# Opening an mLSTM layer by quarters of the inner dimension, and deferring the closings of its heads

## The chip, the cores and the metric

One core of a Trainium2 chip. Its engines are TensorE (PE: matmuls, with weight loads listed as PEld), VectorE (DVE), ScalarE (ACT), GpSimd (POOL) and SyncE (SP), which here issues the DMA transfers. The metric is the device time of one execution of the whole program in microseconds; the median of three runs of the kernel before is 1912.3 us (1907.47 to 1912.42).

## What is computed

Two sequences, a prompt of 256 positions and a sample of 512, go through the same two-layer encoder of width 1024. The kernel puts them side by side: positions 0 to 255 are the prompt, 256 to 767 the sample.

```python
def trunk(x, c, ...):
    for l in range(DEPTH):
        mod = jax.nn.silu(c) @ adaln_w[l] + adaln_b[l]
        sh1, sc1, g1, sh2, sc2, g2 = [t[:, None, :] for t in jnp.split(mod, 6, axis=-1)]
        h = rmsnorm(x, norm_g[l, 0]) * (1 + sc1) + sh1
        if l % N_MIXERS == 0:
            y = mlstm_mixer(h, mlstm_w_in[j], mlstm_b_gate[j], mlstm_head_g[j], mlstm_w_out[j])
        else:
            y = swa_mixer(h, attn_w_in[j], attn_sink[j], rel_bias, attn_w_out[j])
        x = x + g1 * y
        h = rmsnorm(x, norm_g[l, 1]) * (1 + sc2) + sh2
        x = x + g2 * conv_ffn(h, ffn_w_up[l], ffn_conv_w[l], ffn_conv_b[l], ffn_w_down[l])
    return rmsnorm(x, final_g)
```

Layer 0 has the mLSTM mixer: four heads with queries, keys and values of width 256, gates that run along the sequence in both directions, a root-mean-square norm of each head's output, an output gate (sigmoid) and an output projection. Layer 1 has windowed attention. Every product of fp32 operands is made of three: each operand is split into a high part, rounded, and a low part, the rest, and high x high, low x high and high x low are summed.

## The kernel before

**Layout.** Activations lie with the 1024 model dimensions on partitions, as eight blocks of 128 (`KC`), and positions along the free dimension. `hh` and `hl` (tiles zh and zl in the profile) hold the high and low part of the normed, modulated input. A weight is loaded to a `raw` staging tile (five of them, 512 KB), ScalarE makes its high part `whi` and VectorE its low part `wlo` (`fp_copy_split`, L225 and L226). All matmuls of a product go through `mm`, so they appear as L219.

**Order.** The program is written once in Python, and a scheduler then fixes the order of the instructions on each engine with its own timeline; tile pools with a fixed number of buffers (six `slab`, five `raw`, four PSUM banks `pa` and four `ps`) add waits. Each engine, and SP's queue of transfers, works strictly in that order.

**The start, `first`.** Layer 0 needs the scale and shift of its first norm, a product of the conditioning vector with 2048 columns of `adaln_w`. `adaln` loads these columns in 16 pieces by rows and multiplies each as it comes (32x512 matmuls), then transposes the result. In turn with this, `Norm` runs on the two halves of the sample (`RANGES[0]`, `RANGES[1]`): ScalarE squares (L103), POOL adds five of the eight squares (L107), TensorE sums the remaining three over the partitions (128x2 matmuls against a constant), VectorE and POOL form the root (L125, L126), a matmul broadcasts it, VectorE scales x (L520). Only when all eight blocks of scale and shift are there does `modulate` apply them (L527) and split the result into zh and zl.

**Products of the opening, `mlstm` and `window`.** Three weight units come first: the gates and the two 128-column halves of head 0's queries. `window` runs each over the sample's two halves in 256 columns, then the prompt, whose norm sums all eight squares on TensorE. Head 0's keys follow unit by unit (`gemmT`), in 512 and 256 columns, then its values (`gemmN`).

**Gate chain and heads.** From the gates come scans on VectorE (L632 to L639), a round trip through DRAM (`mrows`) that spreads a row over partitions, and masks added on POOL (L659). For each head, scores of q and k (tile pa) are multiplied by exponentials E and split into PT; these meet the values; VectorE and ScalarE form hs. The closing of a head and sequence follows at once: POOL takes the root of the norm (L773), ScalarE scales hs (L776), TensorE transposes it (L780), VectorE writes it out (L784). After four heads come the output gates (L796, L797).

**Filling.** Two generators are stepped from within this work: `fillp` makes the rest of layer 0's modulation on TensorE (`adaln_g`), `fill` makes all of layer 1's (`adaln_v`), mainly on VectorE (L467, L469: two passes over 1024 columns for each of 48 rows).

## Time and profile before

| | |
|---|---|
| median of three runs | 1912.3 us |
| the profiled execution | 1916.26 us |
| its span, first to last instruction | 1914.1 us |
| mean granted TensorE clock | 0.984 |
| PE busy | 1832.3 us, 96% |
| DVE busy | 1387.7 us, 73% |
| ACT, POOL busy | 908.6 us, 47%; 557.2 us, 29% |

A line of the timeline gives start, duration, engine, source line, operation, output and inputs with their shapes, and in brackets the idle time before it and what ended that. A line of the view by stretches gives the stretch, its length, then busy time and instruction count of PE, PEld, DVE, ACT and POOL, the granted TensorE clock (1.00 is full), the mean busy share of the DMA engines and GB/s. Matmuls are pipelined, so the distance between the starts of two is their cost, and a busy PE may be one that runs slowly.

### The profile page before, as it was taken

The numbers are of one execution on the slowest core, as the hardware profiler recorded it, in microseconds if no ns is written. First come the engines' busy times: TensorE is split into PE (matmuls) and PEld (weight loads), VectorE is DVE, ScalarE is ACT, GpSimd is POOL, SyncE is SP. The second block draws the span as 40 slices with busy tenths as digits, with TensorE's granted clock in tenths as the row PEclk, the third lists the DMA queues.
The fourth block names the chain that finished last, engine by engine and source line by source line (L and its number), as shares of the span: only waits on it lengthen the run. The fifth ranks groups of instructions, "written<-read, shape, count | busy, mean of one in ns | idle before, by whom it ended". The sixth has DMA issues, their size and how long they took to land.

```text
span 1914.1 us, 29110 instructions
## 1 busy us (share of the span) xinstructions
PE 1832.3 (96%) x11270; PEld 1671.3 (87%) x11270; DVE 1387.7 (73%) x2249; ACT 908.6 (47%) x1828; POOL 557.2 (29%) x438
## 2 busy tenths in 40 slices
PE   7999999999999999999999999999899999999997
PEld 4978887879988999999999998779898999999996
DVE  4765577684689777777777765775898777777775
ACT  3444334433555444444444555774564444444443
POOL 2101001022344333333332211332534333333324
PEclk7999999999999999999999999999999999999998
DMA  8344466455212222122223231122222222222211
GB/s 323 113 142 130 148 199 209 159 175 174 70 55 78 67 66 67 66 66 67 66 67 99 84 95 42 46 82 88 78 66 78 67 67 67 66 67 67 67 34 66
DMA packets 63957, 183.43 MB, mean 96 GB/s; under 512 B 6135, under 2 KB 23799, under 8 KB 63820
## 3 DMA queue, kind: packets, MB, share of 16 engines
q1 hardware_dynamic: 63820, 181.58, 29.1%
q8 instruction: 88, 1.44, 0.3%
q14 instruction: 49, 0.40, 0.1%
HBM read 175.13 MB, written 6.43 MB: 95 GB/s over the span
## 4 chain that ended last, share of the span: by engine, by line
PE 83%; DVE 6%; issue 4%; POOL 2%; DMA 2%; ACT 2%; SPq 0%; POOLq 0%; ACTq 0%; DVEq 0%
PE pa L219 26%; PE ps L219 23%; PE ps L1083 10%; PE ps L1084 10%; PE ps L1085 10%; PE pa L941 2%; DVE slab L550 1%; DVE wlo L226 1%; DMA raw<-in_adaln_w_dram 1%; POOL nt L107 1%; PE pa L1083 1%; PE pa L1084 1%; PE pa L1085 1%; ACT whi L225 1%; DMA raw<-in_w_dram 1%
## 5 line engine op out<-in xcount | busy, mean ns | idle before, releaser
L225 ACT CAST whi<-raw 128x1024 fp32r<-128x1024 f32 x243 | 254.6, 1049 | 422.0 <-PE pa L219 204.2
L226 DVE TENSOR_TENSOR wlo<-raw,whi 128x1024 fp32r<-128x1024 f32 x243 | 335.1, 1381 | 137.3 <-ACT whi L225 136.1
L219 PE MATMUL pa<-slab,whi 128*128 128x256 f32 (+1 forms) x1472 | 348.0, 334 | 4.7 <-DVE slab L550 4.6
L219 PEld LDWEIGHTS pa<-slab,whi 128*128 128x128 f32 x1472 | 254.1, 191 | 31.8 <-DVE slab L550 6.2
L550 DVE SCALAR_TENSOR_TENSOR slab<-pa,mod,slab 128x256 f32<-128x256 f32 (+1 forms) x368 | 207.2, 591 | 73.1 <-PE pa L219 73.1
L219 PE MATMUL pa<-slab,wlo 128*128 128x256 f32 (+1 forms) x736 | 234.9, 332 | 0.0
L219 PE MATMUL ps<-zh,whi 128*128 128x256 f32 (+2 forms) x688 | 228.3, 336 | 4.6 <-ACT whi L225 3.5
L219 PE MATMUL ps<-zh,wlo 128*128 128x256 f32 (+2 forms) x688 | 228.4, 335 | 3.4 <-DVE wlo L226 3.4
L219 PE MATMUL ps<-zl,whi 128*128 128x256 f32 (+2 forms) x688 | 229.0, 335 | 0.7 <-DVE zl L513 0.7
L1083 PE MATMUL ps<-zh,whi 128*128 128x384 f32 x504 | 171.0, 339 | 16.2 <-ACT ps L1146 15.2
L1085 PE MATMUL ps<-zh,wlo 128*128 128x384 f32 x504 | 169.0, 335 | 0.0
L1084 PE MATMUL ps<-zl,whi 128*128 128x384 f32 x504 | 168.9, 335 | 0.0
L219 PEld LDWEIGHTS pa<-slab,wlo 128*128 128x128 f32 x736 | 140.1, 191 | 13.0 <-DVE wlo L226 0.6
L1114 POOL TENSOR_TENSOR raw<-raw,raw 128x512 f32<-128x512 f32 x44 | 59.7, 1357 | 312.3 <-DVE wlo L226 263.6
L219 PEld LDWEIGHTS ps<-zh,whi 128*128 128x128 f32 x688 | 131.3, 192 | 17.6 <-ACT whi L225 5.1
L219 PEld LDWEIGHTS ps<-zh,wlo 128*128 128x128 f32 x688 | 131.6, 191 | 14.5 <-DVE wlo L226 4.2
L219 PEld LDWEIGHTS ps<-zl,whi 128*128 128x128 f32 x688 | 131.4, 192 | 11.9 <-issue 1.7
L1235 POOL TENSOR_TENSOR slab<-slab 128x772 f32<-128x772 f32 x44 | 87.5, 1989 | 179.1 <-DVE slab L1186 178.0
L1185 DVE SCALAR_TENSOR_TENSOR slab<-slab,cstt,slab 128x771 f32<-128x771 f32 x88 | 106.7, 1215 | 26.8 <-ACT slab L1183 26.7
L1186 DVE SCALAR_TENSOR_TENSOR slab<-slab,cstt,slab 128x771 f32<-128x771 f32 x88 | 121.0, 1375 | 0.7
L469 DVE SCALAR_TENSOR_TENSOR ada<-raw,silc,ada 128x1024 f32<-128x1024 f32 x84 | 110.3, 1345 | 7.8 <-DMA raw<-in_adaln_w_dram 7.6
L1083 PEld LDWEIGHTS ps<-zh,whi 128*128 128x128 f32 x504 | 94.6, 188 | 24.2 <-ACT ps L1146 20.3
(279 smaller groups left out, 4186.3 us busy)
## 6 DMA issues: line engine op xcount, KB each, us to landing
raw<-in_w_dram SPq DMA_DIRECT2D x206, 512.0 KB, 3.7
raw<-in_adaln_w_dram SPq DMA_DIRECT2D x84, 512.0 KB, 4.3
slab<-in_x_dram SPq DMA_DIRECT2D x12, 512.0 KB, 8.4
slab<-in_adaln_w_dram SPq DMA_DIRECT2D x12, 512.0 KB, 10.3
slab<-mrows SPq DMA_DIRECT2D x8, 384.0 KB, 5.1
xs<-slab SPq DMA_DIRECT2D x6, 512.0 KB, 3.5
bt<-brow SPq DMA_DIRECT2D x16, 192.0 KB, 3.2
slab<-xs SPq DMA_DIRECT2D x6, 512.0 KB, 8.2
```

Source lines behind the costliest of these rows:

```text
L219: self.nc.tensor.matmul(out, lhsT, rhs, start=start, stop=stop)
L225: nc.scalar.copy(hi, src)
L226: return nc.vector.tensor_tensor(lo, src, hi.bitcast(F32), ALU.subtract)
L469: stt(acc[:, s], row, w, acc[:, s], ALU.mult, ALU.add)
L550: self.nc.vector.scalar_tensor_tensor(x, o, self.mod[l][:, gc + c, q : q + 1], x, ALU.mult, ALU.add)
L1083: mm(o, wh[:, k], hi[k], start=start and k == 0, stop=False, skip_group_check=True)
L1084: mm(o, wh[:, k], lo[k], start=False, stop=False, skip_group_check=True)
L1085: mm(o, wl[:, k], hi[k], start=False, stop=k == 3, skip_group_check=True)
L1114: tt(q[0], q[2], q[0], ALU.subtract)
L1185: stt(y[:, 1:], u[:, :-1], w(0), y[:, 1:], ALU.mult, ALU.add)
L1186: stt(y[:, :-1], u[:, 1:], w(2), y[:, :-1], ALU.mult, ALU.add)
L1235: nc.gpsimd.tensor_tensor(y, y, yrow[:, j], ALU.mult)
```

## The change

The modulation's 2048 columns are repacked on the host into an array `ada0` of four quarters; a quarter holds the scale and shift of two of the eight blocks. The sample's x is loaded first, in four transfers, then quarter 0, the gate weight and the two query weights, then quarters 1 to 3, then the prompt's x.

`opening` takes the place of `adaln`, `scaled`, `modulate` and the window. It norms the whole sample at once, with the squares summed on VectorE; other norms keep their sums on POOL. `adaln_z` makes one quarter: eight matmuls, a copy, and four narrow matmuls against a selector `sel` in place of transposes. For each quarter the two blocks are scaled, shifted and split, and the three units are multiplied by these two blocks in 512 columns; the next quarter's modulation matmuls stand between the products of this quarter. Head 0's keys over the sample follow, with the prompt's norm between them (five of its squares are summed on POOL, three sums on TensorE), and then all five units over the prompt. Within `opening`, TensorE, ScalarE and VectorE keep the order in which it is written.

`modulated`, which layer 1's opening norm also uses, writes the low part of a block one block later. A load of ScalarE's exponential table is fixed in program order behind the opening. The closing of a head becomes a generator `close`: the norm's root is taken at once, scale, transposes and write-out later; for the sample behind the prompt's outputs, for the prompt behind the next head's first product (behind the first output gate for the last head). The steps of `fill` and `fillp` are spread anew. The prompt's exponentials are split once per block, not once per direction.

```diff
+    def apart(self, src, pool):
+        w = [[pool.tile([P, 640], R, tag="PT", name=self.nm("wp"), bufs=8)[:, :512] for _ in range(2)] for _ in range(2)]
+        for j in range(2):
+            self.fp_copy_split(w[0][j], w[1][j], src[:, 512 * j : 512 * (j + 1)])
+        return w
...
+    def products(self, o, w, ks, cols):
+        for k in ks:
+            ah, al = self.hh[:, k, cols], self.hl[:, k, cols]
+            self.mm(o, w[0][k], ah, k == 0, False)
+            self.mm(o, w[0][k], al, False, False)
+            self.mm(o, w[1][k], ah, False, k == KC - 1)
+    def opening(self, xt, units, loads, pool, consume):
+        nc = self.nc
+        stt = nc.vector.scalar_tensor_tensor
+        sample = slice(*SEQS[0])
+        x = lambda c: xt[c // 4][:, c % 4, sample]
+        ws, bank = [], []
+        acc = None
+        for c in range(KC):
+            sq = pool.tile([P, 640], F32, tag="PT", name=self.nm("sq"), bufs=8)[:, :512]
+            nc.scalar.activation(sq, x(c), AF.Square)
+            if acc is None:
+                acc = sq
+            else:
+                nc.vector.tensor_tensor(acc, acc, sq, ALU.add)
+        pm = self.pa()
+        for b in range(4):
+            self.mm(pm[:, 2 * b : 2 * b + 2], acc[:, b * P : (b + 1) * P], self.inv, True, True)
+        r = self.nt.tile([P, 4], F32, tag="nr", name=self.nm("nr"), bufs=3)
+        mean = pm[:, :8].rearrange("p (b s) -> p b s", s=2)[:, :, 0]
+        nc.vector.tensor_scalar(r, mean, EPS, None, ALU.add)
+        nc.gpsimd.tensor_tensor(r, r, self.mhalf[:, :4], ALU.pow)
+        turn = self.adaln_z(0, units[0], pool)
+        next(turn)
+        pr = self.pa()
+        for b in range(4):
+            self.mm(pr[:, b * P : (b + 1) * P], r[:, b : b + 1].to_broadcast([P, P]), self.ident, True, True)
+        for _ in range(2):
+            next(turn)
+        for z in range(4):
+            cs = (2 * z, 2 * z + 1)
+            if z == 0:
+                ws.append(self.blocks(self.apart(loads[0], pool)))
+            for c in cs:
+                stt(x(c), x(c), self.gain[0][0][:, c, 0:1], pr, ALU.mult, ALU.mult)
+            for c in cs:
+                sh = self.mod[0][:, c, 0:1]
+                hi = self.hh[:, c, sample]
+                nc.scalar.activation(hi, x(c), AF.Identity, bias=sh)
+                stt(self.hl[:, c, sample], x(c), sh, hi.bitcast(F32), ALU.add, ALU.subtract)
+            if z < 3:
+                turn = self.adaln_z(z + 1, units[z + 1], pool)
+            for i in range(3):
+                if z == 0:
+                    bank.append(self.ps())
+                    if i:
+                        ws.append(self.blocks(self.split(loads[i])))
+                self.products(bank[i], ws[i], cs, sample)
+                if i == 0 and z < 3:
+                    for _ in range(2):
+                        next(turn)
+                if i == 1 and z < 3:
+                    next(turn)
+        norm = Norm(self, xt, PROMPT, self.modulated(0, 0))
+        for c in range(KC):
+            norm.square(c)
+        stages = norm.stages()
+        next(stages)
+        for i in range(2):
+            w = self.load(U_MIN + 1, i)
+            ws.append(self.blocks(self.apart(w, pool) if i else self.split(w)))
+        for i in range(3):
+            consume[i](0, bank[i])
+        bank += [self.ps() for _ in range(2)]
+        self.products(bank[3], ws[3], range(4), sample)
+        next(stages)
+        self.products(bank[3], ws[3], range(4, KC), sample)
+        consume[3](0, bank[3])
+        for _ in stages:
+            pass
+        self.products(bank[4], ws[4], range(KC), sample)
+        consume[4](0, bank[4])
...
+    def quarter_loads(self, z, pool):
...
+            self.nc.sync.dma_start(part, self.io["ada0"][:, u * 1024 : (u + 1) * 1024])
+            out.append(part.rearrange("p (k c) -> p k c", k=2))
+        return out
+    def adaln_z(self, z, units, pool):
...
+        ps = self.pa()
+        for k in range(KC):
+            r0 = 32 * (k % 4)
+            self.mm(ps[r0 : r0 + 32], self.silc[:, k, :], units[k // 2][:, k % 2], k < 4, k > 3)
+            if k == 3:
                 yield
...
+        sb = pool.tile([P, 640], F32, tag="E", name=self.nm("sb"), bufs=2)
+        nc.scalar.copy(sb[:, :512], ps)
+        yield
+        pt = self.pa()[:, :8]
         for b in range(4):
+            self.mm(pt[:, 2 * b : 2 * b + 2], sb[:, b * P : (b + 1) * P], self.sel, True, True)
+        src = pt.rearrange("p (i b s) -> p i b s", i=2, b=2)
+        for i in range(2):
+            c = 8 * i + 2 * z
...
+            ts = []
+            for c in range(KC + 1):
+                if c < KC:
+                    ts.append(self.tmp([P, c1 - c0]))
+                    g = self.gain[l][i][:, c, q : q + 1]
+                    nc.vector.scalar_tensor_tensor(ts[c], x(c), g, pr, ALU.mult, ALU.mult)
+                    nc.scalar.activation(self.hh[:, c, c0:c1], ts[c], AF.Identity, bias=self.mod[l][:, 24 * i + c, q : q + 1])
+                if c:
+                    b = c - 1
+                    self.behind = nc.vector.scalar_tensor_tensor(
+                        self.hl[:, b, c0:c1], ts[b], self.mod[l][:, 24 * i + b, q : q + 1],
+                        self.hh[:, b, c0:c1].bitcast(F32), ALU.add, ALU.subtract,
+                    )
             return ()
         return apply
...
+        nc.gpsimd.memset(B[0:G], 0.0)
...
-        qt0 = self.slab([P, 2, 2, T], R)
-        ws = [(gw, gates)] + [(w, keep(qt0, 0, c)) for c, w in self.halves(U_MIN)]
-        self.load_x(io["x"], RANGES[2:], xt)
+        qk0 = [self.slab([P, 2, 2, T], R) for _ in range(2)]
+        consume = [gates] + [keep(qk0[i], i, c) for i in range(2) for c in range(2)]
+        eng = mybir.EngineType
+        with self.tc.manual_schedule(engines={eng.PE, eng.Activation, eng.DVE}):
+            ws = opening(consume)
+        behind = self.behind
+        self.tc.keep_in_program_order(
+            nc.scalar.preload_act_table_set("natural_log_exp_and_others")
+        )
         nc.sync.dma_start(self.kct[:, P:], io["kc"][:, P : 3 * P])
-        norm = Norm(self, xt, PROMPT, self.modulated(0, 0), KC)
-        for c in range(KC):
-            norm.square(c)
-        self.start(PROMPT, norm.stages())
-        self.window(ws)
-        nc.scalar.preload_act_table_set("natural_log_exp_and_others")
+        for w, f in zip(ws, consume):
+            o = self.ps()[:, :256]
+            self.products(o, w, range(KC), slice(*SEQS[1]))
+            f(1, o)
...
-                if h == 0 and i == 0:
-                    qk.append(qt0)
+                if h == 0:
+                    qk.append(qk0[i])
                     continue
...
                 for c, w in self.halves(U_MIN + 3 * h + i):
                     for q in range(2):
                         keep(t, i, c)(q, self.gemmT(w, q))
-                        if h and (q <= c or h > 1):
+                        if closes:
+                            self.step(closes.pop(0))
+                        if q <= c or h > 1:
                             self.step(self.fill)
-                    if h:
-                        self.step(self.fillp)
+                    self.step(self.fillp)
                 qk.append(t)
...
-                    if t % 2 == 0:
-                        self.step(self.fill)
-                    elif h:
-                        self.step(self.fillp)
+                    if h:
+                        self.step((self.fill, self.fillp)[t % 2])
...
-                        for d, cols in ((0, slice(nb, w)), (1, slice(0, nb))):
-                            m = cols.stop - cols.start
-                            pts[q, j, d] = [self.tmp([P, m], R) for _ in range(2)]
-                            self.fp_copy_split(*pts[q, j, d], E[:, cols])
+                        t = [self.tmp([P, w], R) for _ in range(2)]
+                    self.fp_copy_split(t[0][:, :w], t[1][:, :w], E[:, :w])
+                    pts[q, j, 0] = [x[:, nb:w] for x in t]
+                    pts[q, j, 1] = [x[:, :nb] for x in t]
...
+            def close(h, q, hq, ss):
+                s0, s1 = SEQS[q]
+                t0, t1 = s0 // P, s1 // P
+                nc.vector.tensor_scalar(ss[:, t0:t1], ss[:, t0:t1], 1.0 / 256.0, EPS, ALU.mult, ALU.add)
+                nc.gpsimd.tensor_tensor(ss[:, t0:t1], ss[:, t0:t1], self.mhalf[:, : t1 - t0], ALU.pow)
+                yield
+                for ti, hs in enumerate(hq, t0):
+                    nc.scalar.activation(hs, hs, AF.Copy, scale=ss[:, ti : ti + 1])
+                for c in range(2):
+                    pt = self.pa()
+                    for i, hs in enumerate(hq):
+                        nc.tensor.transpose(pt[:, i * P : (i + 1) * P], hs[:, c * P : (c + 1) * P], self.ident)
+                    ch = 2 * h + c
+                    nc.vector.tensor_scalar(
+                        hsT[ch // 4][:, ch % 4, s0:s1], pt[:, : s1 - s0], self.cst(HG + ch), None, ALU.mult
+                    )
...
                 n = (s1 - s0) // P
-                self.step(self.fillp, 2)
+                self.step(self.fillp)
...
-                    hs = pool.tile([P, 256], F32, tag="hs", name=self.nm("hs"), bufs=4)
+                    if q == 0:
+                        hs = pool.tile([P, 256], F32, tag="hs", name=self.nm("hs"), bufs=4)
+                    else:
+                        hs = self.tmp([P, 256])
...
+                closes.append(close(h, q, hq, ss))
+                next(closes[-1])
+                if q:
+                    self.step(closes.pop(0))
+                with self.tc.issue_after(behind.ins):
+                    self.step(self.fill)
...
                     o = self.gemmT(w, q)
-                    self.step(self.fill)
+                    if closes:
+                        self.step(closes.pop(0))
+                    self.step((self.fill, self.fillp)[q])
+                    if q and c:
+                        self.step(self.fill)
...
+        xt = [self.slab([P, 4, T]) for _ in range(2)]
+        for c in range(0, KC, 2):
+            t0, t1 = SEQS[0]
+            self.nc.sync.dma_start(xt[c // 4][:, c % 4 : c % 4 + 2, t0:t1], x[:, c : c + 2, t0:t1])
+        self.sel = pool.tile([P, 2], F32, name="sel")
+        self.nc.vector.tensor_reduce(
+            self.sel, self.ident.rearrange("p (g s) -> p s g", g=4)[:, 0:2], op=ALU.add, axis=mybir.AxisListType.X
+        )
+        units = [self.quarter_loads(0, pool)]
+        loads = [self.raw(self.io["wg"])] + [self.load(U_MIN, c) for c in range(2)]
+        units += [self.quarter_loads(z, pool) for z in (1, 2, 3)]
+        self.load_x(x, RANGES[2:], xt)
...
+    a0 = inp["adaln_w"][0][:, :2048].reshape(KC, P, 2, 4, 256)
+    arr["ada0"] = np.ascontiguousarray(a0.transpose(1, 3, 0, 2, 4).reshape(P, 4 * 4096))
```

134 lines of the change are left out of this document (29 added, 105 removed).

## The prediction

> **What bounds the kernel now.** I read the page's shares of engine time first, then the chain of work that ended last, then the stretches (busy time of each engine, granted TensorE clock, DMA).
>
> ```profile
> PE 1832.3 (96%) x11270; PEld 1671.3 (87%) x11270; DVE 1387.7 (73%) x2249; ACT 908.6 (47%) x1828; POOL 557.2 (29%) x438
> ...
> PE 83%; DVE 6%; issue 4%; POOL 2%; DMA 2%; ACT 2%; SPq 0%; POOLq 0%; ACTq 0%; DVEq 0%
> ```
>
> ```profile
> 0.00:10.00 10.00, 0.00 (x0) 0.00 (x0) 0.46 (x4) 5.45 (x11) 2.38 (x7) 1.00 0.78 264
> 10.00:20.00 10.00, 9.47 (x48) 3.13 (x48) 2.90 (x9) 0.01 (x1) 2.17 (x3) 1.00 1.02 391
> 20.00:30.00 10.00, 7.02 (x30) 3.17 (x28) 3.37 (x3) 3.66 (x9) 4.26 (x6) 0.70 1.03 414
> 30.00:40.00 10.00, 9.20 (x49) 5.11 (x41) 7.33 (x24) 4.28 (x14) 0.08 (x1) 0.67 1.05 397
> 140.00:160.00 20.00, 16.03 (x105) 13.26 (x104) 8.85 (x24) 10.62 (x33) 8.98 (x6) 0.91 0.53 161
> 160.00:400.00 240.00, 235.17 (x1671) 202.85 (x1670) 166.78 (x284) 96.81 (x253) 19.43 (x12) 1.00 0.52 170
> 400.00:500.00 100.00, 96.01 (x546) 87.26 (x545) 56.45 (x79) 32.57 (x58) 23.88 (x19) 0.97 0.44 148
> 500.00:1914.00 1414.00, 1361.54 (x8158) 1267.10 (x8156) 1071.84 (x1705) 710.05 (x1356) 489.07 (x383) 0.99 0.22 69
> ```
>
> TensorE carries 83% of the chain. A change pays where TensorE has no useful work or runs at a lower clock: the first 45 us, where the DMA runs full (391 to 414 GB/s) and few matmuls run, the end of the first head (16.03 busy of 20), and 4.8 and 4.0 us of idle in 160:400 and 400:500. After 500 us the changed kernel's instruction lists are the same but for a few places around layer 1's opening norm, so I give that stretch nothing. The opening in the timeline, TensorE's lines mainly:
>
> ```profile
> 13.36 1.69 PE L219 MATMUL pa<-inv,nt 128*128 128x2 f32 x12
> 14.97 1.06 PE L219 MATMUL ps<-raw,silc 128*32 128x512 f32 x8
> 15.08 0.16 DVE L125 TENSOR_SCALAR nr<-pa 128x2 f32<-128x2 f32 x1 [13.78 <-PE pa L219]
> 16.09 0.71 PE L219 MATMUL pa<-kct,nr 128*128 128x128 f32 x4
> 23.23 3.20 PE L219 MATMUL ps<-slab,silc 128*32 128x512 f32 x8 [2.89 <-DMA slab<-in_adaln_w_dram]
> 29.02 1.93 PE L219 MATMUL ps<-slab,silc 128*32 128x512 f32 x8
> 38.42 5.28 PE L219 MATMUL pa<-inv,nt 128*128 128x2 f32 x24
> 40.72 1.04 ACT L225 CAST whi<-raw 128x1024 fp32r<-128x1024 f32 x1
> 43.57 0.56 PE L219 MATMUL ps<-zh,whi 128*128 128x256 f32 x1
> 44.40 1.22 DVE L226 TENSOR_TENSOR wlo<-raw,whi 128x1024 fp32r<-128x1024 f32 x1
> 62.06 0.28 PE L219 MATMUL ps<-zh,whi 128*128 128x256 f32 x1
> 63.14 0.28 PE L219 MATMUL pa<-zh,whi 128*128 128x256 f32 x1
> 71.66 0.28 PE L219 MATMUL pa<-zh,wlo 128*128 128x256 f32 x1
> 72.94 0.39 PE L219 MATMUL ps<-zh,whi 128*128 128x512 f32 x1
> 77.25 0.39 PE L219 MATMUL ps<-zl,whi 128*128 128x512 f32 x1
> ```
>
> Products run steadily from 43.57; at 63.14 the three opening units (gates and the two halves of head 0's queries) are done for the sample sequence and those of the prompt begin. From 62.06 to 71.66 stand 80 matmuls of 256 columns, 0.12 us apart; from 72.94 to 77.25, 19 of 512, 0.227 apart. The clock:
>
> ```profile
> 24.00:34.00 10.00, 9.92 (x42) 4.67 (x44) 3.25 (x8) 1.04 (x1) 2.09 (x3) 0.50 1.04 398
> 38.00:48.00 10.00, 9.94 (x46) 9.65 (x47) 10.00 (x28) 7.46 (x21) 0.89 (x1) 0.50 0.46 165
> 44.00:46.00 2.00, 2.00 (x11) 2.00 (x11) 2.00 (x5) 1.46 (x5) 0.00 (x0) 0.50 0.00 0
> 50.00:52.00 2.00, 2.00 (x20) 2.00 (x19) 0.00 (x0) 0.00 (x0) 0.40 (x1) 1.00 0.59 217
> ```
>
> At clock 0.50 eleven products go in 2 us, at 1.00 twenty. Products from 43.57 on brought the full clock back at about 48, 4.4 us later.
>
> **The change, part by part.** *Landing of the transfers.* The opening stays bound by DMA, so I carry the bytes over: 2.64 MB moved by 10 us, 6.55 by 20, 10.69 by 30, 14.66 by 40. The transfer TensorE awaited at 23.23 is the 13th of 0.52 MB (7.15 MB with the constants) while 7.9 MB had moved: one lands when 0.74 MB more than its own sum have moved. New order: sample x (2.43 MB), quarter 0 (4.53), gate and two query weights (6.10), quarters 1 to 3 (8.20, 10.3, 12.4), prompt x. Landings: x 11.4, quarter 0 16.7, gate weight 18.1, quarter 1 25.8, quarter 3 36.1 us. The three weights, moved ahead of quarter 1 on SP's queue, cost that quarter 1.57 MB, 3.8 us.
>
> *Up to the first product.* Eight squares of 512 on ScalarE with the sums on VectorE follow the landings. VectorE's and ScalarE's times for 512 columns are those of the old sample evictions:
>
> ```profile
> 60.46 0.60 ACT L228 ACTIVATE slab<-ps 128x512 fp32r<-128x512 f32 x1 [1.50 <-PE ps L219]
> 63.06 0.68 DVE L229 SCALAR_TENSOR_TENSOR slab<-ps,slab 128x512 fp32r<-128x512 f32 x1
> ```
>
> After x: two squares 1.2, last sum 0.7, eight passes of the column sum 1.1 (12 took 1.69), root and its way to TensorE 1.35 (1.0 from 15.08 to 16.09, and by my estimate a third more for four columns instead of two), broadcast 0.7: 16.5. Quarter 0's last part 16.7 + 0.5; copy 0.8; eight selecting passes 1.1; three small VectorE steps 0.6: 19.7. Ahead of the modulation VectorE's list has two halves of the gate weight's split, 1.3; then modulation 0.7 and the cast 0.6: first product at **22.4** instead of 43.57. The low parts come 0.8 and 1.5 later, so the first six products end at 24.3.
>
> *Four quarters, TensorE in written order.* Behind the first six stand quarter 1's modulation matmuls (landing 25.8), behind those the products of the second unit. ScalarE has the copy of that modulation ahead of the query weight's cast: 26.3 + 0.8 + 1.04 = 28.1, VectorE's low part 29.4. TensorE did little from 17 to 28, so I take clock 0.50 there, as the row 24:34 has it: second unit until 31.1, selection 1.8 until 32.9, third weight's low part only at 34.7, third unit until 36.4, quarter 1's first unit until 39.0. From 34.7 TensorE is dense, so the clock is full from about 39. A quarter then costs 18 x 0.227 + 1.06 + 1.1 = 6.3 us, and 1.1 of waiting for scale, cast and low part in a row (selection to first product 2.1, covered by the third unit's 1.36): 46.4 after quarter 2's first unit, 53.8 after quarter 3's, **56.5** at the end of the three units, against 63.1: -6.6.
>
> *Rest of the opening.* Before, from 63.1: 72 x 0.12 for the prompt and 16.7 for the key weights = 25.3. After, from 56.5: 48 x 0.227 for the keys, 120 x 0.12 for the prompt = 25.3, plus the prompt's column sums, now in this stretch, 1.7, the broadcast 0.5, and the key weight's low part 0.5. Opening: **-3.9**. Ends: if the clock is full all along, 3 us better; if semaphore hops that I took as 0.1 to 0.2 are double, 3 worse.
> *Nothing for* two things with a cover:
>
> ```profile
> 7.66 3.94 POOL L107 TENSOR_TENSOR nt<-nt,nt 128x256 f32<-128x256 f32 x5 [7.22 <-ACT nt L103]
> 70.46 1.28 ACT L626 ACT_TABLE_LOAD   x1
> 85.27 0.68 DVE L639 TENSOR_TENSOR_SCAN slab<-slab 4x256 f32<-4x256 f32 x1
> 109.25 4.46 PE L219 MATMUL pa<-slab,slab 128*128 128x512 f32 x18
> ```
>
> The prompt's squares now have five sums on POOL; the key products and ScalarE's casts lie over them, bare they are 3.9. The table load at 70.46 stands in the gate chain and goes, but TensorE's products lie over that chain (last scan done at 86, first score at 109). Its new place: the gates are out at 76, scans by 96, masks 106, weights of head 0 split by 116, while TensorE reaches the outputs at about 120. If that cover is gone the whole lateness counts (rival 2). Fewer splits of the scores (8 instead of 16 for the prompt) and a memset moved to POOL lie on engines with room. The later low parts in the shared modulation: one 0.4 us step either way.
>
> *Closings.* Where TensorE waited from the first head's end to the end of the stage:
>
> ```profile
> PE pa L780 <- ACT hs L776: 3.9, 2, 3.3
> PE ps L219 <- DVE wlo L226: 3.4, 4, 1.4
> PE ps L219 <- ACT whi L225: 2.6, 2, 1.4
> ```
>
> The 3.3 is the first head's sample closing: the norm's scale, then transposes. Deferred, it has the prompt's outputs in front (18 x 0.12 = 2.2), so about 1.5 us remain; the clock dip there (0.91 over 20 us, 1.8 us) should halve: **-2.5** (ends 0 and -5.1). The next waits are for weight splits at later heads' ends, 6.0 us, where VectorE and ScalarE now do closing work. The change takes some of it away but adds filling steps there: 39 of the layer-1 modulation's 49 steps are called before the output gates, 34 now. I take **-2** (ends -6 and +8).
>
> Sum: 3.9 + 2.5 + 2 = 8.4. The profiled execution took 1916.3 (span 1914.1); the median is 1912.3, 0.2% under it. 1912.3 - 8.4 = **1904**.
>
> **The rivals.** *1, slower: the splits queue behind the filling.* Each filling step is two VectorE instructions:
>
> ```profile
> L469 DVE SCALAR_TENSOR_TENSOR ada<-raw,silc,ada 128x1024 f32<-128x1024 f32 x72 | 95.4, 1355 | 0.8 <-DMA raw<-in_adaln_w_dram 0.7
> ```
>
> Five more steps are 5 x 2 x 1.36 = 13.6 us more on VectorE in the heads, in less time, and each holds one of five staging buffers that the next weights need. If all of it ends as waits for splits at three heads' ends, -6.4 + 13.6 = +7: 1919. It decides once these waits pass 18 us in place of 6. Against it: VectorE is busy 167 of 240 us in 160:400.
>
> *2, the gate chain takes the opening's gain.* Head 0's weights come at 116 against TensorE's 120: 4 us of slack, and scans wait in VectorE's queue behind splits and filling. If they come 8 us later, the opening's 3.9 is gone and 1908 is left.
>
> *3, the clock stays at half through the quarters.* The waits of 1 us in each quarter, the narrow selections and the DMA could keep it down. From 39.0 on TensorE's 4.9 + 6.3 + 4.1 us of work would double, less 2 of covered waits: +13, so 1917. Against it: eleven half-speed products per 2 us did release it. The Trainium skill, "TensorE: Matmul & The Clock Gate", section "HAM oscillation", speaks for this rival: bursts of matmuls shorter than the wait for the next slice are re-throttled at every slice. By that rule each quarter would start cold, which is the 1917 above. The trace agrees as far as idle time goes: the clock fell to 0.50 by 24 us after the 2.9 us wait ahead of 23.23; but the waits I count after 36 are about 1 us.
>
> *4, more is freed.* The clock is full in the opening (-3) and all waits at heads' ends go (-6): 1895.
>
> *5, the change doesn't do what it says:* only the sample's opening norm moves its sums to VectorE; the other norms' lists still add on POOL. That is counted as nothing above and changes no time.
>
> **How the numbers follow.** Forecast 0.42, rival 4 0.20, rival 1 0.16, rivals 2 and 3 0.11 each. What a measurement of this kernel can tell from no change is about 0.3%, 5.7 us: 1906.6 to 1918.0. Faster: the forecast and rival 4, 0.62; same: rivals 2 and 3, 0.22; slower: rival 1, 0.16. Range 1891 to 1916: from rival 4 with 4 us more for the closings' own bound, up to just under rivals 1 and 3; the forecast's own is 1898 to 1908.
>
> **What would show it.** First product near 22 and the three units done near 56; clock 0.50 until about 39, 1.00 afterwards; key products for the prompt done near 84.5; first outputs of head 0 near 120 without a wait for the score weights; the transposes' wait at most 1.5 us; waits for weight splits in the heads under 6 us. Wrong if the quarters cost over 8 us each, if TensorE waits for head 0's weights, or if the waits for splits pass 15 us.

## The result, and the profile after

The changed kernel took **1932.9 us** (median; 1932.9 to 1934.2) against 1912.4 for the kernel before: 1.0115 times as long, interval 1.0097 to 1.0132. A second measurement beside later experiments gave 1929.2 us and 1.0088 (1.0059 to 1.0118). Forecast were 1904 us and a gain. The sign was wrong, and the time lies outside the range.

The page of the changed kernel shows TensorE with nearly the same busy time and the same place at the head of the chain (80% against 83%); VectorE's share of the chain rose from 6% to 8%:

```profile
PE 1835.4 (95%) x11190; PEld 1666.7 (86%) x11190; DVE 1383.2 (72%) x2224; ACT 907.0 (47%) x1806; POOL 554.4 (29%) x433
...
PE 80%; DVE 8%; issue 3%; ACT 3%; POOL 3%; DMA 2%; SPq 0%; POOLq 0%; ACTq 0%; DVEq 0%
```

To say where the time went, I use one row that both kernels have: the first column sums of the norm that follows layer 0's output projection. Up to there the two programs differ; behind it their instruction lists are the same but for a few places. First the timeline of before, then of the changed kernel:

```profile
490.69 2.06 PE L219 MATMUL pa<-inv,nt 128*128 128x2 f32 x18
```

```profile
509.94 2.06 PE L219 MATMUL pa<-inv,nt 128*128 128x2 f32 x18
```

I call this start S. It came 19.3 us later (a second profile of the changed kernel has 509.7), and the whole span is 17.0 longer (1931.1 against 1914.1). So the loss was made before S. The stretches of the changed kernel (length; busy time of TensorE, weight loads, VectorE, ScalarE, GpSimd; granted clock; DMA share; GB/s):

```profile
30.00:40.00 10.00, 7.54 (x32) 4.22 (x24) 2.49 (x5) 2.48 (x3) 0.00 (x0) 0.67 0.97 370
40.00:50.00 10.00, 9.67 (x44) 6.20 (x45) 3.64 (x9) 1.97 (x3) 0.00 (x0) 0.75 0.18 54
...
160.00:400.00 240.00, 229.63 (x1564) 196.06 (x1564) 157.43 (x269) 89.92 (x233) 14.08 (x10) 0.98 0.47 153
400.00:500.00 100.00, 93.84 (x566) 81.59 (x566) 57.90 (x79) 34.82 (x65) 26.83 (x20) 0.98 0.58 185
```

TensorE's idle time in 160:400 grew from 4.8 to 10.4 us and in 400:500 from 4.0 to 6.2, although VectorE was busy for less of 160:400 than before (157.4 against 166.8). More waiting with no more work: the order in the queues has to be read, not the shares. The granted clock counts too: it stands at 0.98 in 160:400 where the kernel before had 1.00.

**The opening.** TensorE's timeline of the changed kernel:

```profile
13.57 1.86 PE L219 MATMUL pa<-inv,sq 128*128 128x2 f32 x8 [13.57 <-DVE sq L334]
17.23 2.08 PE L219 MATMUL pa<-kct,nr 128*128 128x128 f32 x8
21.90 1.05 PE L219 MATMUL pa<-sel,sb 128*128 128x2 f32 x8 [0.74 <-ACT sb L481]
26.09 0.79 PE L219 MATMUL ps<-zh,wp 128*128 128x512 f32 x1 [3.14 <-ACT zh L358]
33.83 0.50 PE L219 MATMUL ps<-zh,whi 128*128 128x512 f32 x1 [1.66 <-ACT whi L225]
59.85 0.50 PE L219 MATMUL ps<-zh,wp 128*128 128x512 f32 x1 [0.57 <-ACT zh L358]
92.09 0.28 PE L219 MATMUL ps<-whi,zh 128*128 128x256 f32 x1
```

The first product came at 26.09 instead of the forecast 22.4, the last quarter's first at 59.85, and head 0's values (whi,zh) began at 92.09. I call the start of the values V. In the kernel before, V came 3.0 us sooner:

```profile
89.06 0.39 PE L219 MATMUL ps<-whi,zh 128*128 128x256 f32 x1 [0.46 <-DVE slab L226]
```

ScalarE's timeline of the changed kernel at the second unit:

```profile
32.25 0.59 ACT L481 COPY sb<-pa 128x512 f32<-128x512 f32 x1 [5.55 <-PE pa L219]
32.73 2.00 ACT L225 CAST whi<-raw 128x1024 fp32r<-128x1024 f32 x2
```

ScalarE stood idle for 5.55 us ahead of the copy of quarter 1's modulation, and the cast of a weight that could have been made meanwhile is written behind that copy. TensorE then waited for the cast (1.66 at 33.83).

**The heads.** The chain of what held the end of this stage, by line, for before (60 to 490 us) and then for the changed kernel (60 to 510):

```profile
by line: PE ps L219 57.4%; PE pa L219 13.7%; issue 13.0%; DMA raw<-in_w_dram 1.9%; DMA raw<-in_adaln_w_dram 1.6%; PE pa L780 1.3%; DVE wlo L226 1.1%; POOL slab L659 0.9%; DVE ada L469 0.8%; DMA slab<-mrows 0.8%; ACT whi L225 0.7%; DVE ada L
```

```profile
by line: PE ps L219 56.6%; PE pa L219 10.1%; issue 6.6%; DVE ada L558 5.4%; DMA raw<-in_adaln_w_dram 5.0%; DMA raw<-in_w_dram 2.4%; DVE wlo L226 1.7%; DVE slab L839 0.9%; ACT whi L225 0.9%; PE pa L837 0.8%; DVE ada L556 0.8%; ACT nt L103 0.
```

"ada" is the filling (layer 1's modulation on VectorE), "raw<-in_adaln_w_dram" its transfers. In the entries shown, L469 before and L558 after, they went together from 2.4% of the chain to 10.4%. The chain puts down to a transfer all its time from issue to landing, and VectorE can do other work in that time, so such a share is not what VectorE waited. One place, between the second and third heads' ends: the chain's entry, then VectorE's timeline, then TensorE's row in the same view.

```profile
262.87 6.02 DMA raw<-in_adaln_w_dram
```

```profile
259.98 2.48 DVE L558 SCALAR_TENSOR_TENSOR ada<-raw,silc,ada 128x1024 f32<-128x1024 f32 x2 [0.51 <-DMA raw<-in_adaln_w_dram]
...
264.28 2.48 DVE L558 SCALAR_TENSOR_TENSOR ada<-raw,silc,ada 128x1024 f32<-128x1024 f32 x2 [1.21 <-DMA raw<-in_adaln_w_dram]
...
268.98 2.48 DVE L558 SCALAR_TENSOR_TENSOR ada<-raw,silc,ada 128x1024 f32<-128x1024 f32 x2 [1.89 <-DMA raw<-in_adaln_w_dram]
...
271.58 0.68 DVE L810 TENSOR_TENSOR E<-pa,E 128x512 f32<-128x512 f32 x1
```

```profile
272.32 0.97 PE L219 MATMUL pa<-slab,slab 128*128 128x256 f32 x6 [3.50 <-DVE E L810]
```

Three filling steps stand close together on VectorE, with evictions between them. VectorE stood 0.51, 1.21 and 1.89 us for their transfers, and behind the third step stand the products of the third head's score weights (E), for which TensorE waited 3.50 us. A step fetches the row of the next step when it runs, so steps that follow closely stand for their rows. Over the first 520 us the group of these instructions shows, for before and then for the changed kernel, equal work but twice the standing:

```profile
L469 DVE SCALAR_TENSOR_TENSOR ada<-raw,silc,ada 128x1024 f32<-128x1024 f32 x84 | 110.3, 1345 | 7.8 <-DMA raw<-in_adaln_w_dram 7.6
```

```profile
L558 DVE SCALAR_TENSOR_TENSOR ada<-raw,silc,ada 128x1024 f32<-128x1024 f32 x84 | 109.6, 1338 | 15.3 <-DMA raw<-in_adaln_w_dram 15.2
```

TensorE's waits in the changed kernel from 92 to 510 us (sum, times, longest); from head 0's end on, weight splits take no more than before (4.4 + 1.6 against 3.4 + 2.6), and evictions (L229), a modulation transfer and score weights (2.3 us at head 0, 3.5 at the third head) have joined them:

```profile
PE pa L219 <- DVE E L810: 5.8, 2, 3.5
PE ps L219 <- DVE wlo L226: 4.4, 6, 1.8
PE ps L219 <- DVE slab L229: 3.4, 2, 2.4
PE ps L219 <- DMA raw<-in_adaln_w_dram: 2.1, 1, 2.1
PE ps L219 <- ACT whi L225: 1.6, 3, 0.8
```

From V to S the two kernels have the same number of TensorE instructions, 2604 (the second row counts two more at its edges). Before, then the changed kernel (length, TensorE's busy time, clock, DMA share, GB/s):

```profile
89.06:490.69 401.63, 387.10 (x2604) 0.99 0.50 163
```

```profile
92.09:509.94 417.85, 395.68 (x2606) 0.98 0.49 159
```

The 16.2 us lost here have three visible parts. TensorE's idle time is 7.6 us longer (22.2 against 14.5). The clock stood at 0.50 for 20.5 us instead of 10.2, which by my estimate costs up to 5 us. And the narrow products of layer 0's modulation, called at new places too, kept TensorE busy 2.7 us longer; they stand in 30 groups instead of 22:

```profile
L219 PE MATMUL ps<-raw,silc 128*32 128x256 f32 x256 | 19.5, 386 | 0.0
```

```profile
L219 PE MATMUL ps<-raw,silc 128*32 128x256 f32 x256 | 22.2, 396 | 2.1 <-DMA raw<-in_adaln_w_dram 2.1
```

### The profile page after: what moved, and what is told of

Same layout as the page of the kernel before. It is cut to its first block, busy times and chain, and to the rows that moved or that the text cites. A ratio compares the mean times of both kernels' runs of the same rounds, so it can differ in the third digit from the quotient of the medians.

```text
span 1931.1 us, 28919 instructions
## 1 busy us (share of the span) xinstructions
PE 1835.4 (95%) x11190; PEld 1666.7 (86%) x11190; DVE 1383.2 (72%) x2224; ACT 907.0 (47%) x1806; POOL 554.4 (29%) x433
## 4 chain that ended last, share of the span: by engine, by line
PE 80%; DVE 8%; issue 3%; ACT 3%; POOL 3%; DMA 2%; SPq 0%; POOLq 0%; ACTq 0%; DVEq 0%
PE pa L219 25%; PE ps L219 23%; PE ps L1181 10%; PE ps L1182 9%; PE ps L1183 9%; PE pa L1039 2%; DVE wlo L226 1%; DVE ada L558 1%; DMA raw<-in_adaln_w_dram 1%; DMA raw<-in_w_dram 1%; DVE slab L631 1%; POOL nt L107 1%; ACT whi L225 1%; PE pa L1181 1%; PE pa L1182 1%
## 5 line engine op out<-in xcount | busy, mean ns | idle before, releaser
L219 PE MATMUL ps<-zh,whi 128*128 128x256 f32 (+2 forms) x656 | 223.2, 344 | 8.5 <-ACT whi L225 4.2
L219 PE MATMUL ps<-zh,wlo 128*128 128x256 f32 (+2 forms) x656 | 222.7, 342 | 5.7 <-DVE wlo L226 5.7
L219 PE MATMUL ps<-zl,whi 128*128 128x256 f32 (+2 forms) x656 | 223.2, 341 | 0.7 <-DVE zl L605 0.7
L219 PEld LDWEIGHTS ps<-zh,whi 128*128 128x128 f32 x656 | 126.4, 194 | 26.6 <-ACT whi L225 7.4
L219 PEld LDWEIGHTS ps<-zh,wlo 128*128 128x128 f32 x656 | 126.8, 194 | 19.4 <-DVE wlo L226 8.7
L219 PEld LDWEIGHTS ps<-zl,whi 128*128 128x128 f32 x656 | 127.1, 194 | 11.8 <-issue 1.7
L558 DVE SCALAR_TENSOR_TENSOR ada<-raw,silc,ada 128x1024 f32<-128x1024 f32 x84 | 109.6, 1338 | 15.3 <-DMA raw<-in_adaln_w_dram 15.2
L1181 PEld LDWEIGHTS ps<-zh,whi 128*128 128x128 f32 x504 | 94.9, 188 | 25.0 <-ACT ps L1244 21.2
## 6 DMA issues: line engine op xcount, KB each, us to landing
slab<-in_ada_dram SPq DMA_DIRECT2D x12, 512.0 KB, 10.2
```

The lines of the kernel that those rows point to most:

```text
L219: self.nc.tensor.matmul(out, lhsT, rhs, start=start, stop=stop)
L558: stt(acc[:, s], row, w, acc[:, s], ALU.mult, ALU.add)
L1181: mm(o, wh[:, k], hi[k], start=start and k == 0, stop=False, skip_group_check=True)
```

## The experiments

Two numbers are given for each: the median over the runs with its ratio to before on the same chip (interval in brackets), and S of the profiled execution, which says how much of the time lies before the common part. From S to the end the profiles took 1416 to 1429 us with nearly the same instructions, at mean clocks of 0.979 to 0.990, so a single total says less than S. S itself carries the clock of the opening, so V is given beside it: before and closings_only have the same instructions in the same order on every engine up to V, yet V is 89.1 in one and 87.0 in the other, where the clock didn't fall at 24 us.

**Which part costs it.** Four kernels with parts exchanged (the edits are cut to a few lines). With the old opening the heads of the change were put into the kernel before.

```diff
 # open_alone: in the changed kernel
-                    self.step(self.fillp)          # fill/fillp calls, closings and
-                closes.append(close(h, q, hq, ss)) # split of E as in the kernel before
+                for _ in close(h, q, hq, ss):
+                    pass
 # fill_back: only the fill/fillp calls as before; close_back: only the closings as before
```

> The changed opening with the heads, the closings, the filling steps and the splits of the scores as before. Theory O (the opening itself, by its half clock and the late gate chain, costs the 20 us): 1928 or more. Theory F (the filling steps at their new places cost some 15 us, the opening 4): about 1916. Theory C (the deferred closings cost 15): about 1916 too.

> The opening as before with the changed heads (closings deferred, filling steps at their new places, merged splits). Theories F and C: about 1928, the old 1912 and some 15. Theory O: 1912 to 1916, the heads cost next to nothing.

> The changed kernel with the filling steps called where they were before, all else changed. Theory F: 1916 to 1919. Theories O and C: 1930 or more.

> The changed kernel with every closing done at once at its head's end, all else changed. Theory C: 1917 to 1920. Theories F and O: 1930 to 1936, and by the prediction's step on closings (-2.5) 1935.

Two more complete the table on the old opening:

> The kernel before with closings deferred and the prompt's splits merged, filling steps and opening as before. By the prediction's step: 1910 (-2.5). By the part runs (closings add some 2 us at the new opening with old filling): 1912 to 1915.

> The kernel before with the filling steps at their new places, all else as before. If the new places uncover the filling by themselves: 1918 to 1924, start of the output norm 496 or later. If it needs the deferred closings or the new opening: 1912 to 1915.

| opening | closings deferred | filling at new places | V, us | S, us | median, us | ratio |
|---|---|---|---|---|---|---|
| old | no | no (before) | 89.1 | 490.7 | 1911.6 to 1914.3 | 1 |
| old | yes | no (closings_only) | 87.0 | 487.7 | 1910.4 | 0.9991 [0.9975, 1.0007] |
| old | no | yes (filling_only) | 91.5 | 491.8 | 1920.0 | 1.0036 [1.0019, 1.0053] |
| old | yes | yes (heads_alone) | 91.7 | 497.8 | 1918.8 | 1.0037 [1.0021, 1.0053] |
| new | no | no (open_alone) | 96.1 | 492.3 | 1920.8 | 1.0048 [1.0031, 1.0064] |
| new | yes | no (fill_back) | 95.1 | 494.7 | 1917.5 | 1.0032 [1.0013, 1.0051] |
| new | no | yes (close_back) | 90.1 | 497.8 | 1921.3 | 1.0043 [1.0029, 1.0057] |
| new | yes | yes (changed kernel) | 92.1 | 509.9 | 1932.9 | 1.0115 [1.0097, 1.0132] |

(The merged split of the prompt's scores goes with the deferred closings in the old-opening rows and in the last three.) None of the three theories holds: each part put back takes 12 to 18 us of S off, and no part alone costs that much. At S the parts do not add: on the old opening closings and filling together cost 497.8 - 487.7 - 491.8 + 490.7 = 9 us more than the sum of both, on the new one 9.7; counted from V to S, so without the opening, 6.7 and 6.8. The deferred closings by themselves show -3.0 at S, but 2.1 of it stands at V already, ahead of any closing; 0.8 is left behind V, and the total resolves neither. New places of the filling move two things, layer 1's modulation on VectorE and the narrow products on TensorE: the group of 256 takes 19.3 or 19.5 us in the four kernels with the old places and 21.8 to 22.4 in the other four. No run takes one of them alone to its new places. The totals of open_alone and filling_only lie some 4 us higher than their S lets expect; that isn't explained (open_alone's profiled execution, 1912.6, was the fastest of its ten).

**Is it the filling, and what of it?** One kernel thins the filling's work on VectorE, one removes its transfers, one holds it out of head 0's gate chain; the changed kernel was measured again beside them.

```diff
 # thin_fill
-                    stt(acc[:, s], row, w, acc[:, s], ALU.mult, ALU.add)
+                    stt(acc[:, s, :128], row[:, :128], w, acc[:, s, :128], ALU.mult, ALU.add)
 # no_transfers
-        fetch = lambda grp, k: self.raw(self.io["adaln_w"][...])
+        fetch = lambda grp, k: self.hh[:, 0:2, :512].bitcast(F32)
 # gate_clear: every self.step(self.fill) of the heads
+                    if h == 0:
+                        behind = last        # the last product with E on VectorE
+            with self.tc.issue_after(behind.ins):
```

> The changed kernel once more, as the yardstick of the runs beside it, since each of the four part runs lies only 0.3 to 0.5% over before: 1928 to 1936 under every theory.

> The changed kernel, each accumulating VectorE instruction of the filling (layer 1's modulation) on 128 of its 1024 columns, transfers unchanged; the modulation is left incomplete. Theory D (the filling's time on VectorE, 1.28 us an instruction, holds the gate chain and the weight splits): 1911 to 1917. Theory T (its transfers, which hold staging buffers that the weights need, and which VectorE awaits in order): 1926 or more.

> The changed kernel, the filling's VectorE instructions at full size but reading resident data, so its 48 transfers and their staging buffers are gone (the modulation is not computed). Theory T: 1911 to 1917. Theory D: 1926 or more. If both this and the thin filling come to 1917, the two act together (an instruction stands and waits for a late transfer).

> The changed kernel with no filling step before the last score product of head 0 on VectorE. If the filling does its harm in head 0's gate chain (five steps stand there, the first scores' products wait 5.8 us): 1921 to 1926. If it does it at the later heads' ends: 1930 or more.

| kernel | V, us | S, us | median, us | ratio |
|---|---|---|---|---|
| changed kernel again | 92.4 | 509.7 | 1929.2 | 1.0088 [1.0059, 1.0118] |
| thin_fill | 90.1 | 491.5 | 1915.5 | 1.0021 [1.0003, 1.0038] |
| no_transfers | 92.7 | 502.6 | 1922.4 | 1.0057 [1.0039, 1.0075] |
| gate_clear | 90.9 | 509.5 | 1931.5 | 1.0110 [1.0088, 1.0131] |

Taking away either half of the filling brings S forward: 18.4 us without most of its time on VectorE (2.0 of them at V already), 7.3 without its transfers. The two overlap, since their sum is more than the whole 19.3. Theory D fits the larger part; no_transfers fell between the two forecasts. How long VectorE stands for the transfers is not the measure of the harm: in thin_fill it stood 29.9 us for them, twice as long as in the changed kernel, and S is 491.5.

In gate_clear no step stands before head 0's score weights, and TensorE's wait for them (2.3 of the 5.8 us that the expectation put there) is gone. S is unchanged even so: at the first head's end TensorE now waits 8.5 us in five pieces (144 to 157 us) where the changed kernel waits 3.1. So taking the steps out of the gate chain alone gains nothing; the waits came back later.

**Was it hidden before?** The same thinning in the kernel before:

> The kernel before with each accumulating filling instruction on 128 of 1024 columns; the modulation is left incomplete. If the filling was hidden before (theory U: the change uncovers it): 1907 to 1912, start of the output norm 486 to 491. If it cost as much before: 1893 to 1898, start near 472.

S 478.3, median 1900.7 us, ratio 0.9936 [0.9917, 0.9955]. So the filling wasn't hidden before either: its VectorE time was worth 12.4 us of S there and is worth 18.4 now. Neither forecast of this run holds; the change made a cost larger that was there already. But the pair says more. With the filling thinned in both, the changed kernel is still 13.2 us later at S (491.5 against 478.3), and 12.1 of that lies between V and S (thin_before, then thin_fill):

```profile
88.94:478.29 389.35, 382.35 (x2605) 1.00 0.51 168
```

```profile
90.07:491.49 401.42, 389.37 (x2607) 0.99 0.50 164
```

So what the filling's VectorE time costs more than before accounts for 6.0 of the 19.3 us at S, 4.2 of the 16.2 behind V. In the thinned pair TensorE's idle time is 5 us longer in the changed kernel (12.1 against 7.0), and its narrow products take 23.6 us instead of 19.5.

**Does it help to hold the steps back?** Each step was ordered behind the eviction or split written just before its call.

```diff
 # pinned
+            with self.tc.issue_after(self.last.ins):   # last low part written on VectorE
                 self.step(self.fill)
```

> The changed kernel, each filling step of the heads and output gates ordered on VectorE behind the low part of the eviction or split written just before its call; number of steps and their transfers unchanged. Theory H (the scheduler draws steps forward, where they stand with late transfers ahead of weight splits, score products and closings): 1911 to 1918, the start of the output norm near 495 instead of 509.9. If the steps cost the same wherever they stand: 1927 or more, the start near 510.

S 520.8, median 1942.5 us, 1.0160 [1.0135, 1.0185]: worse by 11 at S. My theory H, that the scheduler does the harm by drawing steps forward, fell. VectorE stands 0.0 us for the filling's transfers in this kernel, the slowest at S so far, so that standing isn't the cause either. TensorE's waits in this kernel from 125 to 480 us have other names again:

```profile
PE ps L219 <- ACT whi L225: 6.4, 5, 2.7
PE ps L219 <- DMA raw<-in_adaln_w_dram: 6.1, 2, 3.3
PE pa L845 <- ACT nt L841: 3.0, 3, 1.8
```

**Without VectorE.** Layer 1's modulation done as layer 0's later groups are, by narrow products on TensorE, with the old filling calls and the deferred closings:

```diff
-        self.fill = self.adaln_v(1, pool)
+        # adaln_g(1, 0..5) chained behind adaln_g(0, 2..5) in self.fillp
+        self.fill = self.fillp
```

> The opening as before, deferred closings, layer 1's modulation by products on TensorE (as layer 0's remaining groups) instead of by VectorE. Theory V (the filling's harm is its time in VectorE's queue): the 12 us of the thin filling less some 8 of additional TensorE work (192 narrow products of 0.06 to 0.08 us in place of 48 of 0.12): 1904 to 1909, start of the output norm 481 to 486. If TensorE then stands for late transfers instead: 1913 or more.

> The same with the changed opening, weight splits ahead. Theory V with the mended opening worth 2 to 3 us: 1901 to 1908, start 478 to 485. If the new opening costs with the closings whatever the filling does (5 us in the part runs): 1908 to 1913.

S 509.2 and 508.7, 1932.3 and 1929.9 us, 1.0106 [1.0085, 1.0128] and 1.0102 [1.0077, 1.0128]. As a gain it failed. The waits (fill_pe, 65 to 505 us) still say something:

```profile
PE ps L219 <- ACT whi L225: 10.0, 3, 8.4
PE ps L433 <- DVE sb L429: 2.6, 5, 0.6
```

The waits for VectorE went from 8.9 us in closings_only to 3.4; one wait of 8.4 for a cast on ScalarE came instead, at the output projection behind the last of the modulation. The products cost far more than I put down, though. Their group of TensorE's instructions, 256 before, now reads:

```profile
L219 PE MATMUL ps<-raw,silc 128*32 128x256 f32 x640 | 48.8, 391 | 0.0
```

That is 384 more, at 0.076 us (48.8/640) 29 us instead of some 15, since each call stands as two.

**The opening, mended.** With the old heads, the splits of the first three weights were written ahead of the copies of the modulation.

```diff
 # open_ahead
         next(turn)
+        ws.append(self.blocks(self.apart(loads[0], pool)))
         pr = self.pa()
...
-                    if i:
-                        ws.append(self.blocks(self.split(loads[i])))
+                    if i == 0:
+                        ws += [self.blocks(self.split(loads[u])) for u in (1, 2)]
```

> The changed opening with the heads as before, and the splits of the first three weights put ahead of the modulation's copy (gates) and of the next quarter's copy (queries) on ScalarE and VectorE. Theory Q (the written order of ScalarE and VectorE made the first product 3.7 and the second unit 4.4 us late): first product near 24.9 instead of 26.1, three units done near 59.4 instead of 63.3, 4 us less than the changed opening with old heads (1920.8): 1915 to 1918. Theory K (TensorE's half clock and late transfers set the opening): no change, 1920.

> The opening with weight splits ahead and the old heads, a second time: start of the output norm 485 to 489 as in its first profile (487.3) if its 3 us over before are real, and then 1909 to 1913; 490 or later and 1915 or more if the first profile was lucky.

> The changed kernel with the pinned filling steps and with the weight splits ahead. By theories H and Q together: 1907 to 1914. By neither: 1927 or more.

S 487.3 and 488.6, 1915.5 and 1914.1 us, 1.0021 [1.0002, 1.0040] and 1.0012 [0.9995, 1.0029]; "both" (with the pinned steps) S 514.9, 1940.8 us, 1.0135 [1.0097, 1.0174]. Against the same kernels without it the mend is worth 5.0 and 3.7 us at S (492.3 without) and 5.9 (520.8 without). Theory Q fits. Theory K isn't wholly apart from it, since the mended openings also ran less at half clock ahead of V (6.8 and 13.7 us against 17.1 in open_alone). S was as forecast the second time, the total 1 us above its forecast. One more thing stood in these profiles: TensorE's row of the last quarter, then VectorE's rows of that moment (open_ahead).

```profile
56.41 0.72 PE L219 MATMUL ps<-zl,wp 128*128 128x512 f32 x1 [4.40 <-DVE zl L358]
```

```profile
53.02 2.20 DVE L555 TENSOR_SCALAR ada<-raw,silc 128x1024 f32<-128x1024 f32 x2 [1.66 <-DMA raw<-in_adaln_w_dram]
55.14 2.35 DVE L358 SCALAR_TENSOR_TENSOR zl<-slab,mod,zh 128x512 fp32r<-128x512 f32 x2
```

With the filling called at its old places, its first step was scheduled into the opening, ahead of the last quarter's low parts, and TensorE waited 4.4 us. open_alone and fill_back have the same wait (4.39). The change's own ordering of the filling behind the prompt's modulation prevents this. With that ordering put around the old calls:

```diff
 # ahead_guard: open_ahead, and around each self.step(self.fill) of the heads
+            with self.tc.issue_after(behind.ins):
```

> The changed opening with weight splits ahead, heads as before, and the filling steps of the heads ordered behind the prompt's modulation, so that none stands inside the opening. If the opening's gain was hidden only by the filling step in it (4.4 us of waiting for the last quarter's low part): start of the output norm 483 to 485 against 487.3 and 488.6 with the step inside and 490.7 before, and 1904 to 1909 in all. If the step only costs elsewhere instead: 487 or more, 1911 to 1915.

S 483.8, as forecast; median 1910.5 us against 1914.3 beside it, 0.9984 [0.9968, 1.0001], 1.5 us above the band forecast for the total. It is the best S of the kernels that do the whole computation, 6.9 under before and 26.1 under the changed kernel; in the total the interval still touches 1. Of the 6.9 us 5.7 stand at V (83.4 against 89.1), while the clock alone moved V of the old opening by 2.1. It also mends the reading of the table: without the wait of 4.4 the new opening with the old heads would stand near 488 at S, so by this estimate the filling's new places cost some 10 us on the new opening (497.8) and 1 on the old. Its opening:

```profile
23.73 0.80 PE L219 MATMUL ps<-zh,wp 128*128 128x512 f32 x1 [2.06 <-ACT zh L357]
...
51.16 0.50 PE L219 MATMUL ps<-zh,wp 128*128 128x512 f32 x1 [0.55 <-ACT zh L357]
...
83.41 0.28 PE L219 MATMUL ps<-whi,zh 128*128 128x256 f32 x1
```

## Why the prediction was wrong, step by step

*Up to the first product: 22.4 forecast, 26.09 measured.* The transfers and VectorE's sums came as forecast (column sums from 13.57). What failed is the sum of TensorE's own small passes in their written order: eight column sums took 1.86 instead of 1.1, the broadcast 2.08 instead of 0.7 (the 0.7 was a row of two calls; four calls stand as eight rows), and quarter 0's modulation matmuls took 1.93 + 1.92, of which the sum had only 0.5. They were done at 21.2 instead of 17.2. From there on the sum is right: the split of the gate weight, copy, selection and scaling took 4.9 against 5.2. With the split ahead the first product came at 23.73 to 24.91.

*Four quarters: three units done at 56.5 forecast.* In the changed kernel 59.85 and 18 products of 0.227 behind it and two waits make 64.7, later than the 63.1 of the kernel before. The failed step is "ScalarE has the copy of that modulation ahead of the query weight's cast: 28.1". I saw that order and priced it as if the copy came at 26.3; it came at 32.25, behind products that began 3.7 us late, took 3.2 us at half clock and not 1.9, and behind modulation matmuls of 2.9 us that the sum had at 0.5. In ahead_guard the last quarter began at 51.16, so the units were done at about 56, as forecast, but by two errors that cancel: a quarter took 8.5 us and not 7.4, and the clock was full from 28.6 us, not 39.

*Rest of the opening: keys' products done at 84.5 forecast.* 92.1 in the changed kernel (+3.0 against before instead of -3.9; some 2 us of V come and go with the clock in either kernel), 83.4 in ahead_guard. The end suits the mended order, not the one that was written, and there it is in part luck.

*Closings, -2.5* (its own terms, 1.8 and 0.9, make 2.7). Not confirmed. Alone, the closings show -3.0 at S and -1.7 [-4.8, +1.3] in the total, but only -0.8 from V to S. The transposes' wait did shrink, from 3.9 to 0.4 us, while a wait of 2.6 for ScalarE (dn) came beside it, and the time at half clock behind V was not halved: 13.7 us against 10.2.

*Head ends, -2 with ends -6 and +8.* This is the term that decided. From V to S the changed kernel lost 19.3 - 3.0 = 16.2 us where closings and head ends together were to gain 4.5. I looked only at waits for weight splits and only at five more steps. Those waits did not grow; score weights, evictions, closings and the narrow products waited instead. My range for this term ended at +8, since it priced the five steps' time (13.6 us) alone. It left out that the filling was already costing 12 us where it stood, the narrow products at their new places (2.7 us of TensorE and a wait of 2.1), and the clock behind V (10.3 us more at 0.50).

*The rivals.* Rival 1 had the right side and the right engine but the wrong victim (6.0 us of waits for splits, as before), and its 13.6 us were less than the 16.2 lost. Rival 2: the scans were done at 105.1 instead of 96, and TensorE waited 2.3 us for head 0's score weights, yet gate_clear, free of filling there, gained nothing, so the gate chain alone decides little. Rival 3 was half true: the clock was 0.50 until about 45 us. The Trainium skill, "TensorE: Matmul & The Clock Gate", section "HAM oscillation", speaks of a return to half clock at every slice; the trace shows one return after the products began, within the first two quarters, and six other runs of the same opening don't have it there (the last section). From 45 on the clock held through waits of 0.57 us. Rival 4 did not come (and 1904 - 3 - 4 is 1897, not 1895), and rival 5 concerned no time. Of the three signs of being wrong two came: quarters of 8.5 us and a wait for head 0's weights; waits for splits did not pass 15 us.

*What stays open.* The runs show that the filling's calls, deferred closings and the new opening cost together what none costs alone, and that S comes back to the level of before (491.5 against 490.7) when most of the filling's time on VectorE goes. They don't show why. Of the 16.2 us behind V, 12.1 remain when both kernels' filling is thinned. Why closings and filling together cost 7 to 10 us more than the sum of each, on either opening, was not isolated, nor whether the lower clock is a cause or follows from the waits; no run took the VectorE filling alone to its new places. The merged split of the scores was not tried without the deferred closings on the old opening, nor the other way round on the new one.

## What to carry to other kernels

That its engine has a low share does not make work that fills gaps free: take it out of both kernels, before and after, and measure what is left. The filling's waits for its own transfers did not tell its price here (0.0 us in the kernel with the latest S, 29.9 in one 29 us sooner). Where a written order puts a copy that depends on the bound engine ahead of a cast that depends on nothing, work out when the copy can really run, with the late start of everything ahead of it; moving the independent casts up gave back 4 to 6 us of S here, a part of which may be the clock's. When parts of a change are measured, look in each part run for what the omitted parts had prevented, as the ordering of the filling did for the opening.

## What the runs showed of the hardware that I had not expected

TensorE's granted clock can fall after a shorter pause than I had reckoned with, but need not. Stretches of the changed kernel, then of gate_clear, which has the same opening, then of ahead_guard (length, TensorE's busy time, clock, DMA share, GB/s):

```profile
32.00:34.00 2.00, 0.34 (x5) 1.00 1.02 396
34.00:36.00 2.00, 1.47 (x4) 0.67 1.09 364
36.00:38.00 2.00, 2.00 (x9) 0.50 1.07 412
```

```profile
32.00:34.00 2.00, 0.34 (x5) 1.00 1.00 399
34.00:36.00 2.00, 1.47 (x6) 1.00 1.06 361
36.00:38.00 2.00, 1.56 (x11) 1.00 1.10 405
```

```profile
24.00:28.00 4.00, 4.00 (x14) 0.50 1.03 411
28.00:51.00 23.00, 20.91 (x120) 0.99 0.70 257
```

In the changed kernel the clock rose at about 31 us, five microseconds after the products began; then TensorE idled 1.66 us (before 33.83) and 0.53, and from 35 the clock was 0.50 until about 45. Its second profile and no_transfers show the same. In six other runs of this opening (open_alone, fill_back, close_back, thin_fill, gate_clear, pinned) the same two pauses stand and the clock stayed at 1.00 until 40 us or longer; five of them then had 3.4 us at half clock. V came at 92.1 to 92.7 us in the three and at 90.1 to 90.9 in the four of the six where no filling step stood inside the opening, so this is worth about 2 us of V. In ahead_guard the same products ran without the 1.66 us pause, the clock rose at about 28.6 and stayed up through the later waits, of which the last quarter's, 0.55 us, is shown above.

The Trainium skill, "TensorE: Matmul & The Clock Gate", section "HAM oscillation", warns of pauses of more than about 3.4 us; here a pause of 1.66 us was followed by the fall in three runs of nine, so by these traces a shorter one can be followed by it. What decides whether it is, these runs can't say.
